# Norm factors in PSUM, priority for bank additions, and a queue order for the next group's operands in a Hymba-style decoder step

## The chip, the cores and the metric

The kernel runs on one core of one Trainium2 chip. A core has five engines that run their own instruction queues and meet through semaphores: TensorE (PE in the profile; PEld is its weight load), VectorE (DVE), ScalarE (ACT), GpSimd (POOL) and SyncE (SP), which here only issues DMAs. [...] The metric is the device time of one execution in microseconds. Lower is better.

## The reference

One decoder layer for 2048 prompt tokens and 8 x 4 sample tokens that share the weights, 2080 token columns in all, with D = 1024 and an FFN width of 2688:

```python
h = rmsnorm(x)
proj = h @ w_in                                  # q, k, v, u
attn = sliding_window_attention(q, k, v)         # window 128, sinks, ALiBi
ssm  = gelu(s5(u));  ssm = ssm * sigmoid(ssm @ w_glu + b_glu)
merged = concat(rmsnorm(attn) * g_attn, rmsnorm(ssm) * g_ssm)
x = x + merged @ w_out
up = rmsnorm(x) @ w_up                           # 2 x 2688 columns
c = conv_b + sum(conv_w[i] * buf[:, i : i + L] for i in range(3))   # causal, buf = state and up
a, g = split(c)
x = x + (silu(g) * a) @ w_down
y = rmsnorm(x) * norm_final
```

Everything is float32. The outputs are y and the new states of attention, S5 and convolution.

## The kernel before

Activations are kept transposed: 128 partitions of one feature block, and token columns along the free dimension. Each float32 matrix product is made of three products of reduced-precision parts: an operand is split into a high part (a cast on one engine, line 84 on ACT) and a low part (source less high part, line 87), and `mm3` (lines 92 to 94) adds high x high, high x low and low x high in one PSUM bank. So every operand that a matmul reads costs a cast and a subtraction on other engines.

The stages follow one another: the projections, attention and S5, GLU, then the output projection, and then the FFN in two groups of four token tiles each, each group with an up-projection of 21 units and a down-projection of 21 blocks for each of its token stretches.

A scheduler orders the instructions of each engine. It takes the program order of the Python text as the priority and issues whatever is ready first; `tc.high_priority(offset=n)` moves instructions n places ahead in that order, and `tc.issue_after(ins)` puts what is traced in its block behind `ins` in the queue of ins's engine, without a wait for its end. Every engine then executes its queue in order, and so does SP with its DMAs.

**Output projection** (lines 1148 to 1175). A loop over eight tiles of 260 columns and, in each, eight output blocks m. A block is 24 matmuls into one of four banks of the pool `ps`. Line 1156 fetches the residual `xm` for the block (12 buffers for 8 blocks a tile), line 1160 adds the bank to it and so frees the bank, and line 1161 stores the sum. Between the blocks three pieces of other work are traced:

- `merged_norm` (line 967) makes the operands of the next tile. For each half of the features `rstd` (line 97) sums the squares over the partitions with a matmul by ones (line 101), takes Ln and Exp on ACT and makes one Newton step on DVE (lines 107, 108, 110); four multiplications (line 975) and four splits follow, whose intermediate `mf` has two buffers.
- `ffn_norm` (line 1123) normalises the finished tile: the same `rstd`, then eight multiplications in place in `xm` (line 1128), each with a store to h2scr (line 1129). Only that store frees the buffer of `xm`.
- `merged_sums` (line 958) loads the inputs of the tile after the next (`mt`, two buffers) and adds their squares on POOL.

The matmul by ones writes to one of two banks of the pool `pst`; the factor itself is in SBUF. Two more banks, the pool `psj`, served earlier stages and lie idle here. In tiles 5 and 6 `early_sums` (line 1101) makes sums and differences of normalised tiles for the first FFN group.

**Up-projection.** `unit` (line 1316) computes one column block of both halves for four tiles. It uses seven products of sums of operands in place of eight: the chain of banks `ux` takes A11, S2, S3 and S1 one after another, the banks `u2`, `u3`, `u4` take A12, S4 and A22. The operands are x0, t2, q1 and q0, each with a high and a low part. `conv` (line 1285) applies the convolution and the gate, and stores the activation to actscr. In the first unit of the first group `finish_front` (line 1187) normalises the last tile; it then closes `pst`, opens the two banks `psv` that u3 uses, and loads q0. In the first unit of the second group `last_norm` does the final norm of the tokens that the first down-projection ended with; its sums use a u3 bank (line 1395).

**Down-projection.** `down` (line 1431) takes the 21 blocks of the FFN width one after another: `load_a` fetches the activation's two parts, `load_wd` (line 1411) a weight, which it splits on ACT and POOL, and 24 matmuls follow. Beside the first group's down-projection the generator `prepare(1)` (line 1485) makes the operands of the second group, one step for each block (line 1474): it loads tiles of h2scr, forms sums on DVE (line 1206 is one of them) and splits them. The cc, ca and cb tiles of the units and the loaded activations share ten buffers of the tag c2.

Of the kernel before, what the change touches and what calls it, by code (L numbers as in the profile page):

```python
# [18 lines left out]
P = 128  # L19
# [61 lines left out]
def split(nc, hi, lo, src, hi_eng, lo_eng):  # L81

    if hi_eng is nc.scalar:
        nc.scalar.copy(hi, src)  # L84
    else:
        hi_eng.tensor_copy(hi, src)
    lo_eng.tensor_tensor(lo, src, hi.bitcast(F32), ALU.subtract)  # L87
# [9 lines left out]
def rstd(c, pool, ps_pool, pstag, ss, n, ones, nm):  # L97
# [13 lines left out]
    return r  # L111

# [515 lines left out]
def body(tc, a):  # L628
# [16 lines left out]
    with ExitStack() as top:  # L645
# [321 lines left out]
        def merged_norm(it, mt, ss, ps_pool, tag):  # L967
# [3 lines left out]
            for half in range(2):  # L971
                r = rstd(c, p3, ps_pool, tag, ss[half], n, ones[512], f"m{half}_{it}")
# [128 lines left out]
        def early_sums(pool, sub, k):  # L1101
# [4 lines left out]
            g, v = nc.gpsimd, nc.vector  # L1106
            g.tensor_tensor(b0[:, 0], b1[:, 0], b0[:, 0], ALU.subtract)
            g.tensor_tensor(t2, b1[:, 1], b0[:, 0], ALU.subtract)
            v.tensor_tensor(b1[:, 0], b1[:, 1], b1[:, 0], ALU.subtract)
            v.tensor_tensor(b0[:, 1], b0[:, 1], t2, ALU.subtract)  # L1110
# [4 lines left out]
        with after_preload():  # L1115
# [7 lines left out]
            def ffn_norm(it, xs, ss):  # L1123
                t0, n = TILES3[it]
                r = rstd(c, p3b, pst, "st", ss, n, ones[1024], f"f_{it}")
# [22 lines left out]
            for it, (t0, n) in enumerate(TILES3):  # L1148
# [5 lines left out]
                for m in range(KD):  # L1154
# [5 lines left out]
                    nc.vector.tensor_tensor(xm, xm, pt[:, :n], ALU.add)  # L1160
                    nc.sync.dma_start(x2scr[:, m, t0 : t0 + n], xm)
                    xs.append(xm)
                    if m == 0 and it == 0:
                        sums = merged_sums(1, p3m)
                    if m == (1 if it else 3) and it + 1 < len(TILES3):
                        nxt = merged_norm(it + 1, *sums, pst, "st")
                    if m == 5 and it + 2 < len(TILES3):
                        sums = merged_sums(it + 2, p3m)
                    if m == 2 and old is not None:
                        ffn_norm(*old)  # L1170
# [91 lines left out]
        def load_q(i):  # L1262
            for sub in range(2):
                q = (ffn.q0, ffn.q1)[i][sub] = hi_lo((hb, hd)[i], [2, 4, W], f"q{i}{sub}", 0)
                for k in range(4):
                    s = c2.tile([P, 2, W], F32, tag="c2", name=f"q{i}r_{sub}_{k}")
                    nc.sync.dma_start(s, qscr[:, sub, i, k])
                    split(nc, *[t[:, :, k] for t in q], s, nc.scalar, nc.vector if i else (nc.gpsimd, nc.vector)[k % 2])
# [16 lines left out]
        def conv(ti, j, half, pt, cc):  # L1285
# [22 lines left out]
            if half:  # L1308
# [4 lines left out]
                nc.vector.tensor_tensor(ca.bitcast(F32R), g, cg, ALU.subtract)  # L1313
                nc.sync.dma_start(actscr[:, j, :, t0 : t0 + n], cc[:, :, :n])

        def unit(gi, j, ws, mid):
# [30 lines left out]
            for s in subs:  # L1347
                v.tensor_tensor(c11[s], c11[s], ca[s][:, 0], ALU.add)
                conv(4 * gi + s, j, 0, c11[s], cc0[s])
            products(chain, s2, [ffn.t2[s] for s in subs], False)  # L1350
            for s in subs:
                nc.scalar.copy(ca[s][:, 1], x[s])
            if mid:
                mid()
            p3 = banks(psv, "u3", "u3")
            products(p3, s4, [half(ffn.q1[s], 1) for s in subs])
# [54 lines left out]
        def load_wd(gi, j, t0):  # L1411
# [16 lines left out]
            split(nc, *w, r, nc.scalar, nc.gpsimd)  # L1428
            return w

        def down(gi, beside):

            old = None
            for ti, (t0, n) in enumerate(TILESD[gi]):
# [5 lines left out]
                def load_a(j):  # L1440
                    hl = [dt([P, n], F32R, f"a{i}_{t0}_{j}") for i in "hl"]
                    for i, t in enumerate(hl):
                        nc.sync.dma_start(t.bitcast(F32), actscr[:, j, 1 - i, t0 : t0 + n])
# [186 lines left out]
```

## Time and profile before

| | us |
|---|---|
| median of 3 runs | 2246.32 (2243.3 to 2248.94) |
| the profiled execution, its own time | 2243.47 |
| its span in the trace | 2241.7 |
| PE busy in the span | 2059.5 (92%) |
| DVE, ACT, POOL busy | 1352.0, 1055.4, 1195.8 |

The stages lie in the span like this: the output projection from 547 to 786 us, the first group's up-projection to 1241, its down-projection to 1505, the second group's up-projection to 1952, and its down-projection to the end. In a timeline a row is start, length, engine, line, operation, output <- inputs, shapes and count; brackets hold the idle time of that engine ahead of the row and what ended it. Times are microseconds, means of groups nanoseconds. A matmul's row is longer than the distance to the next, since matmuls overlap; the distance from start to start is what one costs. The granted clock is the share of full speed that TensorE was given.

### The profile page before, as it was taken

To read this page: it belongs to the slowest core of one execution; us is meant where nothing else is said; L and a number is where in the kernel's file an instruction comes from. 1 tells how busy PE (TensorE), PEld (TensorE's weight loads), DVE (VectorE), ACT (ScalarE), POOL (GpSimd) and SP (SyncE) were. 2 spreads that over 40 slices of the span, in tenths; PEclk is the share of its full clock that TensorE was granted. 3 is DMA by queue.
4 is the path that set the end of the run, shared out by engine and by line. 5 is a ranking of instruction groups with operands and counts; after the bars stand their busy time and mean duration, and the time that the engine had idled before them with its cause. 6 is when DMAs were issued, how large, how long until landed. Compare 5 with 4: busy or idle time off the path is not lost.

```text
span 2241.7 us, 41507 instructions
## 1 busy us (share of the span) xinstructions
PE 2059.5 (92%) x14685; PEld 1931.3 (86%) x14685; DVE 1352.0 (60%) x3326; ACT 1055.4 (47%) x2459; POOL 1195.8 (53%) x1168
## 2 busy tenths in 40 slices
PE   8969999978988879999999799998999999889997
PEld 8967878867888879999999687788999999779897
DVE  8859898357678676667667533318666666600231
ACT  6525555674443256666666332225556655611111
POOL 4847775343445456666666443455666666722211
PEclk9989999989999989999999899999999999989998
DMA  7865434785466663333333784744333333573643
GB/s 234 247 160 148 137 104 121 145 237 177 132 207 215 218 214 95 109 106 112 93 116 112 232 283 137 278 149 152 95 110 105 106 98 103 162 204 108 215 129 98
DMA packets 294352, 347.59 MB, mean 155 GB/s; under 512 B 42344, under 2 KB 250864, under 8 KB 294128
## 3 DMA queue, kind: packets, MB, share of 16 engines
q1 hardware_dynamic: 294144, 344.94, 50.7%
q8 instruction: 116, 1.90, 0.4%
q14 instruction: 92, 0.75, 0.1%
HBM read 232.70 MB, written 107.80 MB: 152 GB/s over the span
## 4 chain that ended last, share of the span: by engine, by line
PE 70%; DVE 11%; DMA 6%; issue 4%; ACT 3%; POOL 3%; SPq 2%; DVEq 0%; POOLq 0%; ACTq 0%
PE ux L1328 20%; PE u L1328 15%; PE dn L93 7%; PE dn L94 7%; PE dn L92 7%; DVE xm L1128 2%; PE qkv L92 1%; PE qkv L93 1%; PE qkv L94 1%; SPq L776 1%; PE wo L92 1%; PE wo L94 1%; PE wo L93 1%; PE o L541 1%; PE tp_b L530 1%
## 5 line engine op out<-in xcount | busy, mean ns | idle before, releaser
L87 POOL TENSOR_TENSOR wdl<-wdr,wdh 128x1024 fp32r<-128x1024 f32 x65 | 158.6, 2444 | 306.0 <-ACT wdh L84 280.9
L92 PE MATMUL dn<-ah,wdh 128*128 128x512 f32 (+3 forms) x552 | 205.1, 372 | 19.7 <-DMA ah<-actscr 16.7
L94 PE MATMUL dn<-ah,wdl 128*128 128x512 f32 (+3 forms) x552 | 205.1, 371 | 2.0 <-POOL wdl L87 1.9
L1480 DVE TENSOR_TENSOR xo<-xo,dn 128x512 f32<-128x512 f32 (+3 forms) x40 | 21.9, 584 | 306.0 <-PE dn L94 305.9
L93 PE MATMUL dn<-al,wdh 128*128 128x512 f32 (+3 forms) x552 | 204.6, 371 | 0.1
L84 ACT CAST wdh<-wdr 128x1024 fp32r<-128x1024 f32 x65 | 68.2, 1050 | 273.7 <-PE dn L93 246.3
L1293 ACT ACTIVATE cc<-u,cw 128x260 f32<-128x260 f32 (+1 forms) x252 | 141.3, 563 | 94.3 <-DVE u L1367 67.2
L92 PE MATMUL wo<-mh,wo 128*128 128x260 f32 x512 | 153.5, 300 | 25.8 <-DVE xm L1160 25.8
L87 POOL TENSOR_TENSOR wls<-s,whs 128x1024 fp32r<-128x1024 f32 x42 | 101.2, 2411 | 130.6 <-ACT whs L84 130.6
L1294 DVE SCALAR_TENSOR_TENSOR cc<-u,cw,cc 128x260 f32<-128x260 f32 (+1 forms) x252 | 120.9, 480 | 66.7 <-ACT cc L1293 65.0
L94 PE MATMUL wo<-mh,wo 128*128 128x260 f32 x512 | 150.5, 294 | 0.0
L93 PE MATMUL wo<-ml,wo 128*128 128x260 f32 x512 | 149.9, 293 | 0.0
L92 PEld LDWEIGHTS dn<-ah,wdh 128*128 128x128 f32 x552 | 104.9, 190 | 37.9 <-DMA ah<-actscr 14.8
L1367 DVE TENSOR_TENSOR u<-u,cb 128x262 f32<-128x262 f32 x84 | 36.5, 435 | 155.5 <-PE u L1328 155.5
L92 PEld LDWEIGHTS wo<-mh,wo 128*128 128x128 f32 x512 | 102.9, 201 | 27.5 <-issue 24.6
L92 PE MATMUL qkv<-hh_p,wqh 128*128 128x256 f32 (+1 forms) x384 | 114.3, 298 | 11.7 <-DVE vs L879 7.0
L87 POOL TENSOR_TENSOR wlt<-s,wht 128x512 fp32r<-128x512 f32 x42 | 54.2, 1290 | 131.0 <-ACT wht L84 69.4
L94 PEld LDWEIGHTS dn<-ah,wdl 128*128 128x128 f32 x552 | 104.7, 190 | 19.6 <-POOL wdl L87 3.1
L93 PEld LDWEIGHTS dn<-al,wdh 128*128 128x128 f32 x552 | 105.0, 190 | 17.6 <-DMA al<-actscr 0.8
L1295 DVE SCALAR_TENSOR_TENSOR cc<-u,cw,cc 128x260 f32<-128x260 f32 (+1 forms) x252 | 119.5, 475 | 0.9
L87 POOL TENSOR_TENSOR wlg<-wur,whg 128x1024 fp32r<-128x1024 f32 x42 | 101.3, 2411 | 27.9 <-ACT whg L84 27.9
L92 PE MATMUL dn<-ah,wd 128*128 128x448 f32 (+2 forms) x288 | 94.7, 329 | 23.2 <-DMA ah<-actscr 19.5
(561 smaller groups left out, 8396.5 us busy)
## 6 DMA issues: line engine op xcount, KB each, us to landing
actscr<-cc SPq DMA_DIRECT2D x168, 260.0 KB, 4.9
wur<-in_w_up SPq DMA_DIRECT2D x84, 512.0 KB, 4.2
wdr<-in_w_down SPq DMA_DIRECT2D x77, 512.0 KB, 3.4
x<-in_xT SPq DMA_DIRECT2D x56, 256.0 KB, 3.9
hs<-h2scr SPq DMA_DIRECT2D x44, 262.0 KB, 4.7
ah<-actscr SPq DMA_DIRECT2D x42, 256.0 KB, 4.1
al<-actscr SPq DMA_DIRECT2D x42, 256.0 KB, 3.8
mt<-mscr SPq DMA_DIRECT2D x16, 520.0 KB, 5.1
```

The source lines that it names most:

```text
L84: nc.scalar.copy(hi, src)
L87: lo_eng.tensor_tensor(lo, src, hi.bitcast(F32), ALU.subtract)
L92: nc.tensor.matmul(ps, w[0], x[0], start=first, stop=False)
L93: nc.tensor.matmul(ps, w[0], x[1], start=False, stop=False)
L94: nc.tensor.matmul(ps, w[1], x[0], start=False, stop=last)
L530: nc.tensor.transpose(tp[:, P * j : P * j + P], ss[kv][:, j, P * ch : P * ch + P], c.ident)
L1128: nc.vector.scalar_tensor_tensor(h, xs[k], g_ffn[:, k : k + 1], r, ALU.mult, ALU.mult)
L1293: nc.scalar.activation(cp, pp[:, 2:], AF.Identity, bias=w[3], scale=w[2])
L1294: nc.vector.scalar_tensor_tensor(cp, pp[:, 1 : npr + 1], w[1], cp, ALU.mult, ALU.add)
L1295: nc.vector.scalar_tensor_tensor(cp, pp[:, 0:npr], w[0], cp, ALU.mult, ALU.add)
L1328: nc.tensor.matmul(pt[:, :W], x[p][:, k], y[q][:, k], start=start and k + i == 0, stop=k == 3 and i == 2, skip_group_check=True)
L1367: v.tensor_tensor(c21[s], c21[s], cb[s][:, 0], ALU.add)
```

## The change

1. `merged_norm` in the output projection (from the second tile on) and `ffn_norm` use the new `rstd_psum`: Ln and Exp share one SBUF tile, the Newton step is done in place in the PSUM bank of the sums, and the multiplications read the factor from that bank. The merged factors use the idle pool `psj`.
2. The bank additions of the output projection get priority. `ffn_norm` is traced behind block 1 instead of block 2, `merged_norm` (from the second tile on) behind block 2 instead of block 1.
3. `early_sums` does all four of its operations on POOL.
4. The splits of `load_q` get priority. `finish_front` is called ahead of the S2 products instead of behind them; `last_norm` is called between the two u3 products instead of ahead of both, and each u3 bank is taken just ahead of its product.
5. In `down`, activations are loaded up to three blocks ahead instead of four. A step of the second group's operands is queued behind the last unit's last DVE instruction, and behind the cast, the subtraction and the last activation load that stand ahead of it in the block.

```diff
+def rstd_psum(c, pool, ps, ss, n, ones, nm):
+    nc = c.nc
+    ps = ps[:, :n]
+    nc.tensor.matmul(ps, ones, ss, start=True, stop=True)
+    r0 = pool.tile([P, n], F32, tag="r0", name=f"r0_{nm}")
+    nc.scalar.activation(r0, ps, AF.Ln, bias=c.eps)
+    nc.scalar.activation(r0, r0, AF.Exp, scale=-0.5)
+    nc.vector.scalar_tensor_tensor(ps, ps, EPS, r0, ALU.add, ALU.mult)
+    nc.vector.scalar_tensor_tensor(ps, ps, -0.5, r0, ALU.mult, ALU.mult)
+    nc.vector.scalar_tensor_tensor(ps, ps, 1.5, r0, ALU.add, ALU.mult)
+    return ps
...
-                r = rstd(c, p3, ps_pool, tag, ss[half], n, ones[512], f"m{half}_{it}")
+                if keep:
+                    pt = ps_pool.tile([P, 512], F32, tag=tag, name=f"st_m{half}_{it}")
+                    r = rstd_psum(c, p3, pt, ss[half], n, ones[512], f"m{half}_{it}")
+                else:
+                    r = rstd(c, p3, ps_pool, tag, ss[half], n, ones[512], f"m{half}_{it}")
...
-            v.tensor_tensor(b1[:, 0], b1[:, 1], b1[:, 0], ALU.subtract)
-            v.tensor_tensor(b0[:, 1], b0[:, 1], t2, ALU.subtract)
+            g.tensor_tensor(b1[:, 0], b1[:, 1], b1[:, 0], ALU.subtract)
+            g.tensor_tensor(b0[:, 1], b0[:, 1], t2, ALU.subtract)
...
-                r = rstd(c, p3b, pst, "st", ss, n, ones[1024], f"f_{it}")
+                r = rstd_psum(c, p3b, pst.tile([P, 512], F32, tag="st", name=f"st_f_{it}"), ss, n, ones[1024], f"f_{it}")
...
-                    nc.vector.tensor_tensor(xm, xm, pt[:, :n], ALU.add)
+                    with tc.high_priority(offset=HPD):
+                        nc.vector.tensor_tensor(xm, xm, pt[:, :n], ALU.add)
...
+                    if m == 1 and old is not None:
+                        ffn_norm(*old)
...
-                    if m == (1 if it else 3) and it + 1 < len(TILES3):
-                        nxt = merged_norm(it + 1, *sums, pst, "st")
+                    if m == (2 if it else 3) and it + 1 < len(TILES3):
+                        nxt = merged_norm(it + 1, *sums, psj, "pj", True)
...
-                    if m == 2 and old is not None:
-                        ffn_norm(*old)
...
-                    split(nc, *[t[:, :, k] for t in q], s, nc.scalar, nc.vector if i else (nc.gpsimd, nc.vector)[k % 2])
+                    with tc.high_priority(offset=HPD):
+                        split(nc, *[t[:, :, k] for t in q], s, nc.scalar, nc.vector if i else (nc.gpsimd, nc.vector)[k % 2])
...
-                nc.vector.tensor_tensor(ca.bitcast(F32R), g, cg, ALU.subtract)
+                ffn.last_dve = nc.vector.tensor_tensor(ca.bitcast(F32R), g, cg, ALU.subtract).ins
...
+            if begin:
+                begin()
             products(chain, s2, [ffn.t2[s] for s in subs], False)
             for s in subs:
                 nc.scalar.copy(ca[s][:, 1], x[s])
-            if mid:
-                mid()
-            p3 = banks(psv, "u3", "u3")
-            products(p3, s4, [half(ffn.q1[s], 1) for s in subs])
+            p3 = []
+            for s in subs:
+                if mid and s:
+                    mid()
+                p3 += [psv[s].tile([P, 512], F32, tag="u3", name=f"u3_{gi}_{j}_{s}")]
+                products(p3[s:], s4, [half(ffn.q1[s], 1)])
...
-            split(nc, *w, r, nc.scalar, nc.gpsimd)
+            ffn.last_act, ffn.last_pool = split(nc, *w, r, nc.scalar, nc.gpsimd)
...
-                        nc.sync.dma_start(t.bitcast(F32), actscr[:, j, 1 - i, t0 : t0 + n])
+                        ffn.last_sp = nc.sync.dma_start(t.bitcast(F32), actscr[:, j, 1 - i, t0 : t0 + n]).ins
...
-                    for ahead in range(i, min(i + 4, NF)):
+                    for ahead in range(i, min(i + 3, NF)):
...
-                        next(beside, None)
+                        with tc.issue_after(ffn.last_dve), tc.issue_after(ffn.last_act), tc.issue_after(ffn.last_pool), tc.issue_after(ffn.last_sp):
+                            next(beside, None)
...
-                unit(gi, j, ws, None if j else last_norm if gi else finish_front)
+                unit(gi, j, ws, None if j or gi else finish_front, last_norm if gi and j == 0 else None)
```

`HPD` is 90. `split` now returns its two instructions.

More of the change, by code (lines that the diff above doesn't have):

```diff
@@ L81, in split @@
 def split(nc, hi, lo, src, hi_eng, lo_eng):
[L83 to L87, printed above, removed]
+    i = nc.scalar.copy(hi, src) if hi_eng is nc.scalar else hi_eng.tensor_copy(hi, src)
+    return i.ins, lo_eng.tensor_tensor(lo, src, hi.bitcast(F32), ALU.subtract).ins
 def mm3(nc, ps, w, x, first, last):
@@ L965, in merged_sums, with merged_norm @@
             return mt, [sumsq(c, p3, mt[4 * h : 4 * h + 4], n, f"m{h}_{it}", nc.gpsimd) for h in range(2)]
-        def merged_norm(it, mt, ss, ps_pool, tag):
+        def merged_norm(it, mt, ss, ps_pool, tag, keep=False):
             n = TILES3[it][1]
@@ L1105, in early_sums @@
             t2 = pool.tile([P, W], F32, tag="t2", name=f"est_{sub}_{k}")
-            g, v = nc.gpsimd, nc.vector
+            g = nc.gpsimd
             g.tensor_tensor(b0[:, 0], b1[:, 0], b0[:, 0], ALU.subtract)
             g.tensor_tensor(t2, b1[:, 1], b0[:, 0], ALU.subtract)
-            v.tensor_tensor(b1[:, 0], b1[:, 1], b1[:, 0], ALU.subtract)
-            v.tensor_tensor(b0[:, 1], b0[:, 1], t2, ALU.subtract)
+            g.tensor_tensor(b1[:, 0], b1[:, 1], b1[:, 0], ALU.subtract)
+            g.tensor_tensor(b0[:, 1], b0[:, 1], t2, ALU.subtract)
             nc.sync.dma_start(t2scr[:, sub, k], t2)
@@ L1312, in conv, with unit @@
                 nc.scalar.copy(cg.bitcast(F32R), g)
-                nc.vector.tensor_tensor(ca.bitcast(F32R), g, cg, ALU.subtract)
+                ffn.last_dve = nc.vector.tensor_tensor(ca.bitcast(F32R), g, cg, ALU.subtract).ins
                 nc.sync.dma_start(actscr[:, j, :, t0 : t0 + n], cc[:, :, :n])
-        def unit(gi, j, ws, mid):
+        def unit(gi, j, ws, begin, mid):
             a11, a12, s2, s4, s3, a22, s1 = ws
```

## The prediction

> **What bounds the kernel now.** I read the busy time by stage, then the waits of TensorE (PE) in the slow stage, then that stage's timeline engine by engine. The first row is the output projection, from its first to its last matmul; columns are stretch, length, busy time of PE, PEld (weight load), DVE (VectorE), ACT (ScalarE) and POOL (GpSimd), granted clock, DMA share and GB/s. The second row is a wait: total, times, longest.
>
> ```profile
> 547.00:786.00 239.00, 208.35 (x1582) 204.87 (x1580) 171.89 (x330) 93.51 (x234) 111.31 (x125) 0.93 0.63 194
> PE wo L92 <- DVE xm L1160: 25.8, 7, 4.8
> ```
>
> PE should be full here and is not: seven times it waits for line 1160, the addition that empties a bank, and the granted clock is 0.93. One such stall, in order of time (start, length, engine, line):
>
> ```profile
> 604.95 0.42 PE L92 MATMUL wo<-mh,wo 128*128 128x260 f32 x1
> 607.77 0.42 PE L93 MATMUL wo<-ml,wo 128*128 128x260 f32 x1
> 608.35 0.28 PE L93 MATMUL wo<-ml,wo 128*128 128x260 f32 x1
> 608.47 0.28 PE L94 MATMUL wo<-mh,wo 128*128 128x260 f32 x1
> 615.22 0.60 PE L101 MATMUL st_f<-ss_f,ones 128*128 128x260 f32 x2
> 614.55 0.43 DVE L107 SCALAR_TENSOR_TENSOR t_m<-st_m,r_m 128x260 f32<-128x260 f32 x1
> 624.05 1.36 DVE L975 SCALAR_TENSOR_TENSOR mf<-mt,vec,rs_m 128x260 f32<-128x260 f32 x2 [0.31 <-POOL ml L87]
> 625.33 6.22 DVE L1128 SCALAR_TENSOR_TENSOR xm<-xm,vec,rs_f 128x260 f32<-128x260 f32 x8
> 625.90 6.00 SPq L1129 DMA_DIRECT2D h2scr<-xm  x8
> 631.95 1.87 SPq L1156 DMA_DIRECT2D xm<-in_xT  x4
> 634.40 0.78 DVE L1160 TENSOR_TENSOR xm<-xm,wo 128x260 f32<-128x260 f32 x2 [1.09 <-DMA xm<-in_xT]
> 634.97 0.56 PE L92 MATMUL wo<-mh,wo 128*128 128x260 f32 x1 [4.79 <-DVE xm L1160]
> ```
>
> This tile starts on PE at about 604.1. The merged norm of the next tile (st_m to mf) comes first, the FFN norm of the old tile (st_f, eight multiplications at 625.33) last. Its stores leave by 631.9, and only behind them does SP fetch four xm tiles, whose buffers those stores free (12 buffers, 8 a tile). The addition at 634.40 waits for that fetch, and PE has waited since 630.18 (634.97 less 4.79). So the chain is old norm, store, refill, addition, bank. After the restart the clock is low: from 604.95 to 607.77 are 13 steps of 0.217 us, against 0.12 from 608.35 to 608.47. Some 15 slow steps cost 15 x 0.097 = 1.5 us. A stall thus costs itself and 1.5 us: 25.8 + 7 x 1.5 = **36.3 us** in the stage.
>
> **Part 1: factors in PSUM.** Means in this stage, by form (busy, mean ns | idle before), and one group of eight from the last tile, where POOL idled from 772.5 to 795:
>
> ```profile
> L1128 DVE SCALAR_TENSOR_TENSOR xm<-xm,vec,rs_f 128x260 f32<-128x260 f32 x56 | 38.8, 761 | 0.0
> L975 DVE SCALAR_TENSOR_TENSOR mf<-mt,vec,rs_m 128x260 f32<-128x260 f32 x56 | 34.4, 651 | 4.8 <-POOL ml L87 4.6
> L1160 DVE TENSOR_TENSOR xm<-xm,wo 128x260 f32<-128x260 f32 x64 | 26.1, 420 | 35.6 <-PE wo L94 18.4 <-DMA xm<-in_xT 17.0
> L108 DVE SCALAR_TENSOR_TENSOR t_f<-t_f,r_f 128x260 f32<-128x260 f32 x7 | 6.2, 881 | 0.0
> L107 DVE SCALAR_TENSOR_TENSOR t_f<-st_f,r_f 128x260 f32<-128x260 f32 x7 | 2.9, 416 | 0.0
> 778.03 3.29 DVE L1128 SCALAR_TENSOR_TENSOR xm<-xm,vec,rs_f 128x260 f32<-128x260 f32 x8
> 795.02 1.10 POOL L1278 TENSOR_TENSOR prevt<-prev,cw 128x336 f32<-128x336 f32 x1 [22.51 <-DVE q11l L87]
> ```
>
> Eight multiplications take 3.29 us with POOL idle and 6.22 beside it. L1160 and L107, which read one operand from PSUM, keep 420 and 416 ns; L108, the same arithmetic with all operands in SBUF, takes 881. So an operation with both tensors in SBUF is held by POOL, and one with a PSUM operand is not. The diff moves r into PSUM, which takes every L1128 and L975 and two of the three factor steps out of this: about 2.9 us per group of eight, and 0.9 per FFN factor chain (0.88 + 0.42 to two of 0.42). The instructions keep their number but one: Ln and Exp now share r0, so the second half's Ln waits for the first half's factor; that lies under four mf. The rows don't show a write of r to PSUM; I take 0.42 us, as L107, with 0.88 as the other end.
>
> [...]
>
> **Part 2: order in the tile.** st_f moves from behind block 2 to behind block 1, the merged norm one block back. Blocks take 24 x 0.12 = 2.9 us, so a warm tile is 8 x 2.9 + 0.6 for the sums' matmuls (st_f's row, 0.60; they overlap their neighbours) = 23.8. From tile start: st_f at 5.8; Ln and Exp by 7.5 (two ACT passes of about 0.4, as L1310's 0.39 below, and the hand-overs); factors by 8.8; eight multiplications by 12.5 with an addition between; last store issued by 13, its refill landed near 15.5. Block 4 ends at 15.5, and PE needs its bank at 23.8. The additions' priority removes the queue ahead of them too. Eight microseconds of room: the bank stall goes.
>
> Next in line is the merged norm: st_m, today ahead of st_f, at 9.0. From t_m at 614.55 to the last mf at 625.41 took 10.9 us beside POOL, nearer 8 without the holding; behind the FFN norm it runs 12.5 to 21, the last ml at 22 against 23.8. Its SBUF tiles mt (two buffers) then refill:
>
> ```profile
> mt<-mscr SPq DMA_DIRECT2D x16, 520.0 KB, 5.1
> ah<-actscr SPq DMA_DIRECT2D x42, 256.0 KB, 4.1
> L1107 POOL TENSOR_TENSOR es<-es,es 128x262 f32<-128x262 f32 x8 | 6.8, 856 | 20.6 <-DMA es<-h2scr 19.1 <-DMA h2scr<-xm 1.5
> ```
>
> Refill 5.1 plus squares and sums of about 4 puts the next tile's second sum at 21 + 9 = 30, 6.2 into a tile that asks for it at 9.0. Under 3 us of room. In tiles 5 and 6 POOL also takes 16 subtractions from DVE, 16 x 0.856 = 13.7 us; there I leave half the stall, and two more us elsewhere: 36.3 - 8 = **28 us** gained in the stage.
>
> **Part 3: the last FFN norm.** It runs in the first up-projection unit:
>
> ```profile
> 799.55 0.60 PE L101 MATMUL st_f<-ss_f,ones 128*128 128x260 f32 x2
> 802.88 0.59 PE L1328 MATMUL u<-q10h,whs 128*128 128x262 f32 x1 [2.73 <-DVE t_f L107]
> 805.69 6.31 DVE L1128 SCALAR_TENSOR_TENSOR xm<-xm,vec,rs_f 128x260 f32<-128x260 f32 x8
> 811.56 0.39 PE L1328 MATMUL u<-q00h,whg 128*128 128x262 f32 x1 [1.07 <-ACT q00h L84]
> 816.11 0.59 PE L1328 MATMUL u<-q00l,whg 128*128 128x262 f32 x1 [4.16 <-POOL q00l L87]
> 787.19 0.36 PE L1328 MATMUL ux<-x00h,whv 128*128 128x262 f32 x1 [1.72 <-DVE xm L1160]
> ```
>
> The statistics move ahead of the S2 products (about 5 us), and the multiplications shorten by 3: q0 can be there 8 us sooner, and 1.07 + 4.16 + 1.5 for the clock go. The price: the u3 bank, freed today by L107, stays with r until the last multiplication. If that lands on the first u3 bank, the 2.73 stays. With a little kept back, **6 us**. The first unit's own wait for the last tile's bank, the chain above once more, also goes: **2 us**.
>
> **Part 4: operands of the second group.**
>
> ```profile
> 1241.67 2.54 DVE L1206 TENSOR_TENSOR hs<-hs,hs 128x262 f32<-128x262 f32 x1
> 1243.94 5.43 SPq L1416 DMA_DIRECT2D wdr<-in_w_down  x2
> 1245.24 0.39 ACT L1310 ACTIVATE u<-cc 128x260 f32<-128x260 f32 x1 [2.89 <-DVE cc L1295]
> 1250.42 0.54 SPq L1443 DMA_DIRECT2D ah<-actscr  x1
> 1255.62 0.80 PE L92 MATMUL dn<-ah,wdh 128*128 128x512 f32 x1 [14.58 <-DMA ah<-actscr]
> 1968.91 0.74 PE L92 MATMUL dn<-ah,wd 128*128 128x448 f32 x1 [16.97 <-DMA ah<-actscr]
> 1426.07 0.50 PE L94 MATMUL dn<-ah,wdl 128*128 128x512 f32 x1 [1.91 <-POOL wdl L87]
> 1440.36 0.63 ACT L84 CAST q01h<-hs 128x524 fp32r<-128x524 f32 x1 [4.23 <-DVE hs L1225]
> ```
>
> In the last unit DVE does L1206 for the next group while its own convolutions wait; ACT's L1310 waits 2.89 for them, a down weight's cast queues behind it, and SP's in-order queue behind that weight's buffer, until ah leaves at 1250.42. Queued behind the unit, L1206 frees 2.5 us and earlier ones some more: **4 us**, bounded by 0 and 7. It can't be the whole 14.58: the second group has nothing beside it and waits 16.97. Behind each down weight, the operand's casts no longer delay the weight's at 1426: 1.91, I take **2**. DVE, ACT, POOL and SP each get the queueing: behind them stand only the next group's loads and splits, wanted by the next units, whose first is at 1516.94 below; their last cast is at 1440.36, long before. Loading three blocks ahead instead of four adds no instruction; blocks take 2.9 us at 256 columns and a load 4.1 (its issue row stands in part 2), so two blocks cover it; nothing, between -3 and +8.
>
> **Part 5: the second group's start.**
>
> ```profile
> 1516.94 1.13 PE L1396 MATMUL st_fo<-ss_fo,ones 128*128 128x512 f32 x2 [2.11 <-DVE ss_fo L122]
> 1520.94 0.39 PE L1328 MATMUL u<-q11h,whs 128*128 128x262 f32 x1 [1.42 <-DVE rs_fo L1401]
> ```
>
> The first u3 product (1.5 us) now covers the first wait, but it used to cover the second: the sums and L1401 end where they did. Nothing, within 1.
>
> **Sum.** 28 + 6 + 2 + 4 + 2 = 42 us. The profiled execution took 2243.47 (span 2241.7), the median is 2246.32; 2246.3 - 42 = **2204**.
>
> **Rivals.** *Half of it*: the merged norm or the SP queue ends last in most tiles and keeps half the stalls, and parts 3 and 4 give 5: 2246 - 18 - 5 = 2223. For it: under 3 us of room. Against: DVE is 172 of 239 us busy and loses some 5 us a tile.
> *Nothing*: the holding stays with r in PSUM. Then the multiplications ahead cost the merged norm 6.2, it ends 6 us late, and PE waits for ml or st_m where it waited for xm: about 2244. Against: 416 beside 881 ns.
> *Slower*: as before, and in tiles 5 and 6 the sums queue behind POOL's 13.7 us of subtractions, so that in-order PE stands at st_m. It decides once st_m is later than the 3.7 us (25.8 / 7) a tile that now is lost; 13.7 over what is there gives 2257.
> *More*: both stages lose every stall, part 4 gives 7: 36 + 10 + 2 + 7 + 4 = 59: 2187.
>
> **Chances.** Forecast 0.58, half 0.22, more 0.10, nothing 0.06, slower 0.04. A measurement tells 0.3% (6.7 us) from no change. Faster 0.90, same 0.06, slower 0.04. The range goes from the far case to a little past half: 2184 to 2230.
>
> **What would show it.** L1128 and L975 near 420 to 490 ns beside POOL; no wait of wo for L1160 above 1 us; the stage near 211 us; q0 waits gone at the first unit; the first down wait near 10 us. Wrong if L1128 stays above 700, if wo waits for ml or st_m, or if ah waits grow in the down blocks.

## The result and the profile after

| | before | after |
|---|---|---|
| median, all runs of both kernels | 2247.63 us (2243.3 to 2255.62, 4 runs) | 2222.76 us (2218.95 to 2224.6, 4 runs) |
| ratio | | 0.9883, 95% interval 0.9852 to 0.9914 |
| profiled execution, span | 2243.47, 2241.7 | 2218.95, 2217.2 |

The change takes 24.9 us off; 2204 was predicted, 42 us less, in a range of 2184 to 2230. Read off the timeline of TensorE (PE) by its own stages, the two profiled executions stand so (us). A group's first unit is counted here up to the second product of the next unit (the one into `u2`), because PE waits there for a bank that the first unit frees:

| stage | before | after | difference |
|---|---|---|---|
| output projection, first to last matmul | 238.2 | 216.4 | -21.8 |
| wait ahead of the first unit | 1.7 | 5.5 | +3.8 |
| first unit | 42.6 | 37.5 | -5.0 |
| rest of the up-projection | 411.3 | 408.5 | -2.8 |
| wait ahead of the first down block | 14.6 | 10.1 | -4.5 |
| first group's down-projection | 249.9 | 256.6 | +6.7 |
| second group's first unit | 34.6 | 32.8 | -1.8 |
| the rest of the span | 701.5 | 700.4 | -1.1 |

The output projection starts 2.0 us later in the second, behind code that the change leaves alone; with this the rows add up to the 24.5 us between the spans.

The line numbers have moved: the bank addition is now L1176 (it was L1160), the FFN multiplications L1143 (L1128) with their stores L1144, the merged multiplications L990 (L975), the fetch of xm L1171, the factor steps L119 to L121, `mm3` L89 to L91. First the stage's row (length, PE, PEld, DVE, ACT, POOL busy, granted clock, DMA share, GB/s):

```profile
549.00:766.00 217.00, 203.50 (x1582) 198.49 (x1581) 137.25 (x311) 90.61 (x232) 115.96 (x141) 0.97 0.70 215
```

DVE is busy for 137 us where it was for 172; some 11 of these 35 us were the 16 subtractions of the early sums (L1109 and L1110, 4.1 and 7.1 us), which POOL does now. The granted clock rose from 0.93 to 0.97. PE's waits from here into the first unit:

```profile
PE ux L1345 <- DVE xm L1176: 5.5, 1, 5.5
PE wo L90 <- POOL ml L84: 3.6, 6, 1.5
PE st_f L115 <- DVE ss_f L133: 3.3, 2, 2.7
PE st_m L115 <- POOL ss_m L133: 3.2, 2, 1.6
PE wo L89 <- ACT mh L83: 2.0, 2, 1.4
PE wo L89 <- DVE xm L1176: 0.9, 1, 0.9
```

The 25.8 us of waits for the addition are 0.9. But waits for ml, mh and st_f have come, 8.9 us together, where one of 0.7 was; st_m waited before too (3.7). In this stage PE now waits for operands and sums, and hardly for banks. DVE's groups in the stage, by form:

```profile
L1176 DVE TENSOR_TENSOR xm<-xm,wo 128x260 f32<-128x260 f32 x64 | 26.6, 418 | 24.3 <-DMA xm<-in_xT 12.3 <-PE wo L91 11.5
L990 DVE SCALAR_TENSOR_TENSOR mf<-mt,vec,st_m 128x260 f32<-128x260 f32 x56 | 25.8, 480 | 13.9 <-POOL ml L84 13.7
L1143 DVE SCALAR_TENSOR_TENSOR xm<-xm,vec,st_f 128x260 f32<-128x260 f32 x56 | 23.4, 480 | 0.2
L119 DVE SCALAR_TENSOR_TENSOR st_f<-st_f,r_f 128x260 f32<-128x260 f32 x7 | 3.0, 427 | 0.0
```

761 and 651 ns have become 480, beside a POOL that is busy for 116 us of the stage where it was for 111; the addition, which read a bank before too, takes 418 for 420, and the second FFN factor step, now in the bank (L120), 436 where with all operands in SBUF it took 881. So in these rows POOL holds the operations with both tensors in SBUF, and hardly those with an operand in PSUM. One tile, which begins on PE at 601.4, in the rows of DVE and of SP's DMAs:

```profile
613.37 0.43 DVE L119 SCALAR_TENSOR_TENSOR st_f<-st_f,r_f 128x260 f32<-128x260 f32 x1
614.77 0.48 DVE L1143 SCALAR_TENSOR_TENSOR xm<-xm,vec,st_f 128x260 f32<-128x260 f32 x1
615.51 2.85 DVE L1143 SCALAR_TENSOR_TENSOR xm<-xm,vec,st_f 128x260 f32<-128x260 f32 x7
616.18 3.38 SPq L1144 DMA_DIRECT2D h2scr<-xm  x7
620.11 1.88 SPq L1171 DMA_DIRECT2D xm<-in_xT  x4
```

The FFN norm now comes first: its last store has left by 619.6, and the refill is on its way at 620.1, where it was at 632 for a tile that began at about the same time. Seven multiplications take 2.85 us, and the eight in the first unit below 3.26, against 3.29 for the eight that POOL left alone before: the PSUM source shows no price here. (The 480 ns are the length of one; neighbours overlap.)

Two waits around the first unit were expected to go or to stay small. First, the unit starts late:

```profile
752.89 2.57 DVE L84 TENSOR_TENSOR t21l<-t2r,t21h 128x524 fp32r<-128x524 f32 x1
755.38 2.62 DVE L133 TENSOR_TENSOR ss_f<-ss_f,sq_f 128x260 f32<-128x260 f32 x1
757.92 0.43 DVE L119 SCALAR_TENSOR_TENSOR st_f<-st_f,r_f 128x260 f32<-128x260 f32 x1
765.04 1.89 SPq L1171 DMA_DIRECT2D xm<-in_xT  x4
767.45 0.77 DVE L1176 TENSOR_TENSOR xm<-xm,wo 128x260 f32<-128x260 f32 x2 [3.46 <-DMA xm<-in_xT]
771.17 0.56 PE L1345 MATMUL ux<-x00h,whv 128*128 128x262 f32 x1 [5.49 <-DVE xm L1176]
```

In the last tile splits of t2 and a sum, each of two SBUF tensors and stretched to 2.6 us (0.63 and 0.43 with POOL idle, at 770.94 and 770.26), stand ahead of the FFN norm; factor, stores, refill and addition follow late, the old chain once more. The second wait is inside the unit:

```profile
780.25 0.38 ACT L1359 COPY ca<-ux 128x262 f32<-128x262 f32 x1 [5.22 <-POOL prev L1298]
783.71 0.48 ACT L117 ACTIVATE r_f<-st_f,eps 128x260 f32<-128x260 f32 x1
784.80 0.44 DVE L119 SCALAR_TENSOR_TENSOR st_f<-st_f,r_f 128x260 f32<-128x260 f32 x1
786.22 3.26 DVE L1143 SCALAR_TENSOR_TENSOR xm<-xm,vec,st_f 128x260 f32<-128x260 f32 x8
789.62 0.56 PE L1345 MATMUL u<-q10h,whs 128*128 128x262 f32 x1 [7.22 <-DVE xm L1143]
```

PE waits 7.2 us for the u3 bank that holds the factor, where it waited 2.7; the two q0 waits of 1.07 and 4.16 are gone in return. Last, the first group's down-projection; the first row is its first matmul, the second the start of its second token stretch:

```profile
1227.38 0.79 PE L89 MATMUL dn<-ah,wdh 128*128 128x512 f32 x1 [10.13 <-DMA ah<-actscr]
1353.54 0.47 PE L89 MATMUL dn<-ah,wdh 128*128 128x512 f32 x1 [3.93 <-DMA ah<-actscr]
1377.88 0.51 PE L91 MATMUL dn<-ah,wdl 128*128 128x512 f32 x1 [1.63 <-POOL wdl L84]
1403.32 0.80 PE L91 MATMUL dn<-ah,wdl 128*128 128x512 f32 x1 [1.70 <-POOL wdl L84]
```

### The profile page after: what moved, and what is told of

The parts are those of the page before. It is cut to its first block, busy times and chain, and to the rows that moved or that the text cites. A ratio compares the mean times of both kernels' runs of the same rounds, so it can differ in the third digit from the quotient of the medians.

```text
span 2217.2 us, 41459 instructions
## 1 busy us (share of the span) xinstructions
PE 2055.2 (93%) x14685; PEld 1926.3 (87%) x14685; DVE 1323.1 (60%) x3310; ACT 1054.1 (48%) x2459; POOL 1200.4 (54%) x1184
## 4 chain that ended last, share of the span: by engine, by line
PE 70%; DVE 10%; DMA 7%; POOL 4%; issue 4%; ACT 3%; SPq 2%; DVEq 0%; POOLq 0%; ACTq 0%
PE ux L1345 20%; PE u L1345 16%; PE dn L90 7%; PE dn L91 7%; PE dn L89 6%; DVE xo L1427 1%; PE wo L90 1%; PE wo L91 1%; PE wo L89 1%; PE qkv L89 1%; DMA y<-yscr 1%; PE qkv L91 1%; PE qkv L90 1%; DMA al<-actscr 1%; SPq L787 1%
## 5 line engine op out<-in xcount | busy, mean ns | idle before, releaser
L89 PE MATMUL dn<-ah,wdh 128*128 128x512 f32 (+3 forms) x552 | 205.7, 373 | 17.1 <-DMA ah<-actscr 14.1
L91 PE MATMUL dn<-ah,wdl 128*128 128x512 f32 (+3 forms) x552 | 205.8, 373 | 3.3 <-POOL wdl L84 3.3
L89 PE MATMUL wo<-mh,wo 128*128 128x260 f32 x512 | 149.8, 293 | 2.9 <-ACT mh L83 2.0
L91 PE MATMUL wo<-mh,wo 128*128 128x260 f32 x512 | 147.1, 287 | 0.0
L89 PEld LDWEIGHTS dn<-ah,wdh 128*128 128x128 f32 x552 | 105.6, 191 | 35.4 <-DMA ah<-actscr 10.3
L89 PE MATMUL qkv<-hh_p,wqh 128*128 128x256 f32 (+1 forms) x384 | 114.7, 299 | 13.6 <-DVE vs L890 8.5
L91 PEld LDWEIGHTS dn<-ah,wdl 128*128 128x128 f32 x552 | 105.5, 191 | 20.9 <-POOL wdl L84 4.2
L84 POOL TENSOR_TENSOR wlg<-wur,whg 128x1024 fp32r<-128x1024 f32 x42 | 101.6, 2419 | 28.1 <-ACT whg L83 28.1
L89 PE MATMUL dn<-ah,wd 128*128 128x448 f32 (+2 forms) x288 | 95.0, 330 | 23.0 <-DMA ah<-actscr 19.3
L90 PE MATMUL qkv<-hl_p,wqh 128*128 128x256 f32 (+1 forms) x384 | 111.1, 289 | 0.0
```

Of the source, the lines that this page charges most:

```text
L84: return i.ins, lo_eng.tensor_tensor(lo, src, hi.bitcast(F32), ALU.subtract).ins
L89: nc.tensor.matmul(ps, w[0], x[0], start=first, stop=False)
L90: nc.tensor.matmul(ps, w[0], x[1], start=False, stop=False)
L91: nc.tensor.matmul(ps, w[1], x[0], start=False, stop=last)
```

## The experiments

All start from the changed kernel. The table gives the output projection, the wait ahead of the first unit together with that unit, and the whole run less that of the kernel before in the same set of runs. Of the experiments all but norm_early ran once, with one run of the kernel before beside each set. Eleven runs of the kernel before on one chip lie between 2243.4 and 2253.7 us, so the difference of two single runs is sure to some 10 us only, and stages carry the argument. The output projection is the same code in six of the profiles (after, last_sbuf, begin_early, prev_first, ahead4, no_queue): 216.4 to 222.4, mean 220.0. So a stage is sure to some 3 us, and the 21.8 of the first table are nearer 18, taken from the only profile of the kernel before.

| kernel | output projection | wait + first unit | whole less before |
|---|---|---|---|
| before | 238.2 | 44.3 | 0 |
| after | 216.4 | 43.0 | -24.9 |
| factors_sbuf | 224.4 | 44.2 | -25.8 |
| old_order | 225.1 | 38.4 | -29.6 |
| priority_alone | 244.5 | 43.9 | -3.8 |
| no_priority | 218.9 | 42.3 | -26.0 |
| early_dve | 222.6 | 41.8 | -28.2 |
| memset_pool | 219.7 | 44.2 | -29.0 |
| last_sbuf | 221.4 | 45.4 | -26.7 |
| begin_early | 219.3 | 50.2 | -28.1 |
| prev_first | 221.8 | 40.6 | -30.4 |
| norm_early | 219.9 | 39.7 | -30.5 |
| ahead4 | 218.5 | 43.1 | -25.0 |
| no_queue | 222.4 | 43.0 | -19.7 |

**Which part frees the bank?** The factors back in SBUF, in the new order:

```diff
-                r = rstd_psum(c, p3b, pst.tile([P, 512], F32, tag="st", name=f"st_f_{it}"), ss, n, ones[1024], f"f_{it}")
+                r = rstd(c, p3b, pst, "st", ss, n, ones[1024], f"f_{it}")
...
-                        nxt = merged_norm(it + 1, *sums, psj, "pj", True)
+                        nxt = merged_norm(it + 1, *sums, psj, "pj")
```

> The changed kernel with all norm factors back in SBUF (same order, priorities, pools, queueing). Theory (holding): the multiplications of both norms go from 480 ns back to 650 to 760, the factor steps from 430 to 530 to 880, DVE has some 20 us more in the output projection, and the merged norm becomes late: the stage (216 us from first to last matmul) grows by 10 to 25 us, with waits for ml or st_m. The first unit's u3 wait falls from 7.2 to about 3. Rival (order alone): the order of the two norms made the gain; the stage stays within 4 us of 216 although the multiplications are slow.

The stage takes 224.4, 8 us above the changed kernel's profile and 4 above the mean, so between theory and rival. There is no wait for the addition at all; the waits for ml grew. Its waits and its multiplications:

```profile
PE wo L90 <- POOL ml L84: 8.0, 9, 2.2
PE st_f L98 <- DVE ss_f L133: 4.6, 4, 1.5
```

```profile
L990 DVE SCALAR_TENSOR_TENSOR mf<-mt,vec,rs_m 128x260 f32<-128x260 f32 x56 | 33.2, 620 | 9.5 <-POOL ml L84 8.9
L1143 DVE SCALAR_TENSOR_TENSOR xm<-xm,vec,rs_f 128x260 f32<-128x260 f32 x56 | 28.5, 570 | 0.2
```

So the new order frees the bank also with multiplications that POOL holds, though these are not as slow as before (570 ns for 761). (In the first unit the u3 wait falls to 1.1 us, and q0 is late by 3.6 and 2.5.) Then the old order with the factors in PSUM:

```diff
-                    if m == 1 and old is not None:
-                        ffn_norm(*old)
...
-                    if m == (2 if it else 3) and it + 1 < len(TILES3):
+                    if m == (1 if it else 3) and it + 1 < len(TILES3):
...
+                    if m == 2 and old is not None:
+                        ffn_norm(*old)
```

> The FFN norm of the old tile goes back behind the third block and the next tile's merged norm back behind the second; the PSUM factors, the priority of the additions and everything else stay. Theory (the order made most of the gain; with the factors in SBUF the stage took 224.4 us and no bank wait came back): the chain of stores, refill and addition is late again, the waits of wo for the addition come back with at least 10 of the 25.8 us, and the stage takes 228 to 236 us; whole run 2234 to 2243. Rival (priority and the faster arithmetic are enough in either order): bank waits under 5 us, the stage 216 to 223, and the run within 5 us of the changed kernel.

225.1: the bank waits did come back, 18.0 us of them, and yet the stage is only 5 us longer than the mean, since nothing else waits but st_m (3.5); and the first unit with the wait ahead of it comes out 4.6 us better. Theory and rival each missed half. Over both stretches the old order takes 263.5 us, and the kernels with the new order and the same first unit (after, ahead4, no_queue) 259.4 to 265.4: with the factors in PSUM the new order shows no gain of its own. To see whether the priority, which the last two kernels share, made the gain, both parts were undone together, the two edits above in one; of it here the merged norm:

```diff
                     with tc.high_priority(offset=HPD):
                         nc.vector.tensor_tensor(xm, xm, pt[:, :n], ALU.add)
...
-                    if m == (2 if it else 3) and it + 1 < len(TILES3):
-                        nxt = merged_norm(it + 1, *sums, psj, "pj", True)
+                    if m == (1 if it else 3) and it + 1 < len(TILES3):
+                        nxt = merged_norm(it + 1, *sums, psj, "pj")
```

> Of the change in the output projection only the priority of the additions is left (with the two subtractions on POOL): factors in SBUF, the merged norm first and the FFN norm behind the third block, as before. Before, the stage took 238.2 us; PSUM factors and priority in the old order took 225.1, new order and priority with SBUF factors 224.4, all three 216 to 222. Theory (order and PSUM factors are two ways to the same end, each worth some 13 us without the other, and the priority little): the stage takes 233 to 239 us with 20 us or more of bank waits, the run 2240 to 2255. Rival (the priority is what the two kernels have in common and made the 13 us): the stage takes 222 to 228, the bank waits stay near the 18 us of the old order, and the run ends within 6 us of 2226.

The stage is at 244.5, above the 238.2 of before. Its waits of wo, and its multiplications; then the waits of old_order:

```profile
PE wo L89 <- DVE xm L1176: 33.3, 6, 9.0
```

```profile
L1143 DVE SCALAR_TENSOR_TENSOR xm<-xm,vec,rs_f 128x260 f32<-128x260 f32 x56 | 40.0, 780 | 0.0
```

```profile
PE wo L89 <- DVE xm L1176: 18.0, 6, 4.1
```

From 244.5 the PSUM factors alone take 19.4 us, the order alone 20.1, both 24.5 (to the mean of 220.0): two ways to the same end. What made the stage 6 us longer than before (the priority, or POOL's two more subtractions in the tiles that run up to the wait of 9.0) was not told apart; the subtractions are not all of it, for the waits at 637 and 668 were longer already (5.6 and 5.0 us, before 4.8 and 3.5), and the first early sum is at 675.7. From the changed kernel the priority alone was then taken out:

```diff
-                    with tc.high_priority(offset=HPD):
-                        nc.vector.tensor_tensor(xm, xm, pt[:, :n], ALU.add)
+                    nc.vector.tensor_tensor(xm, xm, pt[:, :n], ALU.add)
```

> The additions of the output projection lose their priority; order, PSUM factors and all else stay. Theory (with the FFN norm first the additions have time enough): the stage stays at 216 to 223 us, with under 5 us of waits for the addition. Rival (without it the additions queue on DVE behind eight multiplications and the statistics, and free their banks late): 5 to 15 us of bank waits, the stage 226 to 235 us.

218.9 and no wait for the addition: in the new order the priority shows no effect.

**What are the new waits?** POOL's two more subtractions go back to DVE:

```diff
-            g.tensor_tensor(b1[:, 0], b1[:, 1], b1[:, 0], ALU.subtract)
-            g.tensor_tensor(b0[:, 1], b0[:, 1], t2, ALU.subtract)
+            v.tensor_tensor(b1[:, 0], b1[:, 1], b1[:, 0], ALU.subtract)
+            v.tensor_tensor(b0[:, 1], b0[:, 1], t2, ALU.subtract)
```

> Of the four subtractions of each early sum, the two that the change gave to POOL go back to DVE; all else stays. Theory (POOL is not late in the two tiles with early sums, DVE loses 16 operations): DVE is held up more, some 16 x 0.5 to 0.8 us = 8 to 13 us more busy in these two tiles, but it waits there for the buffer anyway, so the stage stays within 3 us of 216 to 222. Rival (POOL's 13.7 us of subtractions are what makes the sums and ml late from 628 to 687): the waits of wo for ml in that stretch, 7 us in all, go away, and the stage is 4 to 7 us shorter, 210 to 214.

```profile
PE wo L90 <- POOL ml L84: 6.0, 9, 1.7
```

The stage takes 222.6 and the waits for ml stay, so it is not these two subtractions alone. Next, a wait that stands in DVE's queue in the changed kernel, 4.87 and 2.92 us ahead of the memset of L1102:

```diff
-                nc.vector.memset(s[:, :, NSMP : NSMP + 2], 0.0)
+                (eng or nc.vector).memset(s[:, :, NSMP : NSMP + 2], 0.0)
...
-            b0 = stage(pool, "b0", sub, k, 4, "es0")
+            b0 = stage(pool, "b0", sub, k, 4, "es0", nc.gpsimd)
```

> The small memset of the early sums' first buffer goes from DVE to POOL; all else stays. Theory (DVE stands in order at this memset until a buffer's store has left, 4.87 us at 664 and 2.92 at 669, and so the FFN norm and the merged norm behind it are late): the two DVE waits go, the waits of wo for mh and ml from 681 to 687 (3.7 us and the slow clock behind them) go or fall under 1 us, the stage takes 4 us less than without it. Rival (POOL is late there anyway): the same waits stay, now behind POOL, and the stage is unchanged within 2 us.

The rival held: the stage takes 219.7, as the mean. DVE's two waits went, and its FFN norm ended by 668.4; but the wait moved with the memset:

```profile
670.00 0.10 POOL L1102 MEMSET es<- 128x4 f32 x1 [2.67 <-DMA qscr<-es]
674.01 0.76 POOL L1122 TENSOR_TENSOR es<-es,es 128x262 f32<-128x262 f32 x1 [3.91 <-DMA es<-h2scr]
...
680.23 0.48 DVE L990 SCALAR_TENSOR_TENSOR mf<-mt,vec,st_m 128x260 f32<-128x260 f32 x1 [8.14 <-POOL ml L84]
```

POOL stands in its queue for a buffer and then for a load of the early sums; behind the load come 5.5 us of its own sums and subtractions (674.0 to 679.5) and only then ml, and with two buffers of mf DVE waits 8.1 us for ml. PE's waits for mh and ml from 682 to 690 are no shorter than in the changed kernel. In the tile at 714 the sums of squares are late in the same way, in the changed kernel:

```profile
714.52 0.42 ACT L129 ACTIVATE ss_m<-mt 128x260 f32<-128x260 f32 x1 [1.90 <-DMA mt<-mscr]
714.85 1.02 ACT L132 ACTIVATE sq_m<-mt 128x260 f32<-128x260 f32 x3
716.22 0.98 DVE L133 TENSOR_TENSOR ss_f<-ss_f,sq_f 128x260 f32<-128x260 f32 x1 [2.86 <-ACT sq_f L132]
```

ACT waits 1.9 us for the load of mt, and the FFN's square sq_f stands behind it; st_f then waits 2.66 at 720.16. That was read, not tried.

**The bank in the first unit.** The last norm's factor alone back in SBUF:

```diff
+                if it == len(TILES3) - 1:
+                    r = rstd(c, p3b, pst, "st", ss, n, ones[1024], nm)
+                else:
+                    r = rstd_psum(c, p3b, pst.tile([P, 512], F32, tag="st", name=f"st_{nm}"), ss, n, ones[1024], nm)
```

> The changed kernel with the last tile's FFN factor (the one made in the first up-projection unit) back in SBUF; all else as changed. Theory (bank): the 7.2 us wait of the first u3 product is the PSUM bank that the factor now holds until the last of the eight multiplications; with the factor in SBUF the first factor step frees it and the wait falls to about 3 us (784.80 + 0.44 against 782.40), while the eight multiplications go from 3.3 to 4 to 6 us and q0 comes up to 3 us later, which the s4 and s3 products (6 us) cover. First unit some 3 to 4 us shorter. Rival (late statistics): the wait is set by the late Ln and Exp and stays near 7; the unit is not shorter.

```profile
789.83 0.58 PE L1349 MATMUL u<-q10h,whs 128*128 128x262 f32 x1 [2.88 <-DVE t_f L104]
797.77 0.39 PE L1349 MATMUL u<-q00h,whg 128*128 128x262 f32 x1 [0.42 <-ACT q00h L83]
802.06 0.58 PE L1349 MATMUL u<-q00l,whg 128*128 128x262 f32 x1 [3.90 <-POOL q00l L84]
```

The bank is free at the first factor step and the wait is 2.9; but q0 now is late by 0.4 and 3.9, and the unit takes 40.0 where the changed kernel takes 37.5. In factors_sbuf and priority_alone, where this factor is in SBUF too, it takes 39.6 and 40.4; in the six other experiments whose unit is the changed kernel's, 35.5 to 38.7. So holding the bank is the cheaper side, by 2 to 3 us. Then the norm was begun earlier:

```diff
+            if begin:
+                begin()
             c11 = [t[:, :W] for t in p2]
...
-            if begin:
-                begin()
             products(chain, s2, [ffn.t2[s] for s in subs], False)
```

> The last FFN norm is begun in the first up-projection unit ahead of the additions and convolutions of its first quarter instead of behind them; same instructions. Theory (its factor steps stand on DVE from 777.4 to 784.8 behind the convolutions, and the bank that r holds is free only behind the last multiplication at 789.5): the statistics are on PE already, so the eight multiplications end some 4 to 5 us sooner, the wait of the third quarter's products falls from 7.2 to 2 to 4 us, and the unit's 37.5 us to 32 to 34. Rival (the additions and convolutions put behind the norm are needed as soon): PE waits as long for them, in u2's bank or later, and the unit stays at 36 to 39 us.

```profile
784.92 0.44 DVE L119 SCALAR_TENSOR_TENSOR st_f<-st_f,r_f 128x260 f32<-128x260 f32 x1 [2.32 <-ACT r_f L118]
789.74 0.56 PE L1345 MATMUL u<-q10h,whs 128*128 128x262 f32 x1 [5.15 <-DVE xm L1143]
805.31 0.56 PE L1345 MATMUL u<-q00h,whg 128*128 128x262 f32 x1 [7.00 <-DVE cc L1323]
```

The wait fell to 5.2, and the rival was right with more than it asked: the unit takes 44.8. DVE is free and waits for Ln and Exp, for ACT stands at the copy into ca (5.2 us for POOL, as at 780.25 in the changed kernel). And the convolutions, now behind the norm and q0's splits, keep their bank 7 us too long. So POOL's block was moved ahead of the loads of q1:

```diff
-        load_q(1)
         tailp = up.tile([P, 2 * NF, 2], F32, tag="tailp", name="tailp", bufs=1)
...
         gq.tensor_tensor(prev[:, :, :, 1], prev[:, :, :, 1], wide(3), ALU.add)
+        load_q(1)
```

> The block that loads the earlier steps' convolution inputs and computes with them on POOL is written ahead of the loads of q1 instead of behind them; same instructions. Theory (the last norm is late at the first unit because ACT stands 5.2 us, from 775.0 to 780.2, at the copy into ca, whose buffer that block on POOL holds; Ln and Exp queue behind it, so that the factor is ready only at 785.3 though the sum of squares is there at 776.3): the 5.2 us at the copy go, the factor steps start 2.5 to 4 us sooner, the wait of the third quarter's products falls from 7.2 to 3 to 5 us, and the unit from 37.5 to 34 or 35 us. Rival (the factor steps wait for DVE's convolutions ahead of them in any case): the wait stays at 6.5 to 7.5 us.

```profile
778.18 0.64 ACT L1359 COPY ca<-ux 128x262 f32<-128x262 f32 x2
784.35 0.48 ACT L117 ACTIVATE r_f<-st_f,eps 128x260 f32<-128x260 f32 x1
785.45 0.44 DVE L119 SCALAR_TENSOR_TENSOR st_f<-st_f,r_f 128x260 f32<-128x260 f32 x1
790.27 0.56 PE L1345 MATMUL u<-q10h,whs 128*128 128x262 f32 x1 [5.64 <-DVE xm L1143]
```

The 5.2 us at the copy are gone and the unit takes 35.6, but Ln still stands on ACT behind the convolutions and, at 782.72, a table load of 1.28 us (ACT_TABLE_LOAD): half of the theory, half of the rival. Both moves (of the norm without the loads of q0), with the splits of t2 traced later:

```diff
+                    if it == len(TILES3) - 1 and m == 3:
+                        load_t2()
...
-            with after_preload():
-                ffn_norm(*old)
             pst_close()
...
+            if begin:
+                with after_preload():
+                    ffn_norm(*old)
             c11 = [t[:, :W] for t in p2]
```

> Three moves in one, read stage by stage. (1) The split of t2 goes from the end of the seventh tile to behind the fourth block of the last one; theory: on DVE the splits t21l (2.44 and 2.57 us) and the sum behind them (2.62) stand ahead of the last tile's FFN norm, so its refill lands at 767.4 and the first unit waits 5.5 us; without them that wait falls to 0 to 2.5 us; rival (the refill is late on SP's queue anyway): it stays over 4. (2) The block of earlier convolution inputs ahead of the loads of q1, as in the run of that move alone, where the 5.2 us at the copy into ca went but the factor steps then stood behind DVE's convolutions, and (3) the last norm alone, without the loads of q0, ahead of these convolutions; theory: only both together start the factor early: the wait of the third quarter falls from 7.2 to 1 to 3.5 us and the unit from 37.5 to 32 to 34; rival (the convolutions are needed as soon): a wait for a bank or for cc takes its place, 36 or more. Whole run by the theory 8 to 10 us under the changed kernel, a ratio to before of 0.983 to 0.985; by the rivals 0.988 to 0.990.

Median 2219.9 (6 runs), before 2250.36 (11 runs), ratio 0.9872, interval 0.9849 to 0.9895: no different from the changed kernel's 0.9883. The unit takes 34.4 and its bank wait 3.7, a little outside the theory's figures. The wait ahead of it stayed:

```profile
758.77 1.01 DVE L84 TENSOR_TENSOR t21l<-t2r,t21h 128x524 fp32r<-128x524 f32 x1
759.71 2.63 DVE L133 TENSOR_TENSOR ss_f<-ss_f,sq_f 128x260 f32<-128x260 f32 x1
762.26 0.42 DVE L119 SCALAR_TENSOR_TENSOR st_f<-st_f,r_f 128x260 f32<-128x260 f32 x1
```

But the scheduler put the splits ahead of the factor as before, so the 5.3 us there say nothing of the theory; it is open.

**The down-projection.** Four blocks ahead again, and then the next group's steps without the queueing:

```diff
-                    for ahead in range(i, min(i + 3, NF)):
+                    for ahead in range(i, min(i + 4, NF)):
```

> The changed kernel with activations loaded up to four blocks ahead in the down-projection again; the queueing of the next group's operands stays. The first group's down blocks (first to last matmul) grew from 249.9 to 256.6 us. Theory P (prefetch): three ahead is what costs it; with four they return to about 250, the wait at the second stretch from 3.9 to about 2.2, and the second group's waits for ah and al (2.8 and 2.3) to 2.5 and 1.8. Theory Q (queueing): they stay near 256. The wait between the last unit and the first block (10.1 + 1.4) stays under 12 by P if queueing made it, and returns toward 14.6 if three ahead made it.

```diff
-                        with tc.issue_after(ffn.last_dve), tc.issue_after(ffn.last_act), tc.issue_after(ffn.last_pool), tc.issue_after(ffn.last_sp):
-                            next(beside, None)
+                        next(beside, None)
```

> The changed kernel without the queueing of the next group's operands; three blocks ahead stays. Theory Q: the down blocks return from 256.6 to about 250 and the wait at the first block goes from 10.1 + 1.4 back to about 14.6. Theory P: blocks stay near 256, and if the shorter wait comes from the prefetch it stays near 11.

| | rest of up | wait | down-projection | sum |
|---|---|---|---|---|
| before | 411.3 | 14.6 | 249.9 | 675.8 |
| after | 408.5 | 10.1 | 256.6 | 675.3 |
| ahead4 | 408.6 | 10.8 | 254.1 | 673.5 |
| no_queue | 409.8 | 15.0 | 251.1 | 675.9 |

Without the queueing the wait is back at 15.0, as theory Q said: the queueing takes 4 to 5 us from it. (The 1.3 of the up-projection are not surely its own; last_sbuf, which has it, takes 410.0.) The blocks give part of it back, and four blocks ahead do not prevent that: over the twelve profiles with the queueing they take 249.2 to 256.6 us, mean 253.4, against 249.9 and 251.1 without it. The sum is 668.2 to 675.3 there, mean 672.5; so the queueing is worth some 3 us, at the edge of what these profiles can tell. In the changed kernel PE waits 11.8 us inside the blocks, before 7.1, and the granted clock there is 0.96 for 0.98. Why the blocks take longer is open: the second stretch's wait for ah was 3.9 in the changed kernel and 5.8 with four ahead, against 2.2 before, but 2.1 in last_sbuf, which has the queueing and three ahead. The waits for wdl near 1377 (1.6) come without the queueing too.

## Why the prediction was right, and where its sizes were off

- **The mechanism held**: the bank wait of the output projection was the largest loss, it went, and the result lies within the range. The size did not: 24.9 us are 0.6 of the 42. They are what the half case gave (2223), whose reasons hold in part: the merged norm does end last, but it kept none of the old stalls and brought new ones, and Parts 3 and 4 gave little together. That its number was met so closely is partly luck.
- **Part 1** was right of the operations (480 and 427 ns beside POOL), and the PSUM source showed no price (eight multiplications in 3.26 us, for 3.29 from SBUF with POOL idle). The write to PSUM costs what L119 shows, 0.43. One sum in it was wrong, and nothing was built on it: 0.88 + 0.42 to two of 0.42 saves 0.46 us a factor chain, not 0.9.
- **Part 2**, the order, was right that the refill would come in time, but not with eight microseconds of room: the forecast had it landed 15.5 us into the tile, and it only starts 15.8 us into the second tile and 18.8 to 24.7 into the later ones, which last 25 to 31. By old_order the new order was also not needed beside the factors in PSUM, which the sum did not see. The term that was mis-sized is the stage's 28 us, with 8 kept back for what is late next: 8.9 us of waits for ml, mh and st_f came, and the gain is 18 to 22. PE's waits in the stage fell from 30.2 to 13.0 us, which leaves at most some 5 of the 21.8 for the clock, where the forecast had 10.5. "Under 3 us of room" for the merged norm was the right place. What is late from 655 to 690 is not only the subtractions given to POOL (forecast as 13.7 us, measured 10.8; moving them back showed no gain) but also in-order waits for loads and buffers, on POOL as the memset's run shows, and on ACT by the rows at 714.
- **Part 3**: "the 2.73 stays" became 7.2: the bank was priced by the multiplications alone, and not by the factor's own lateness, behind ACT's copy and DVE's convolutions. The q0 waits went as said, and the unit gained 5.0 of the 6, but not by that account: what the bank took back, the 1.7 at S2 (for a copy into ca) and 1.1 at the next unit's bank made up in part. "The first unit's own wait" fell to the other side: +3.8 for -2; by the rows the factor of the last tile but one is late on DVE, which the run with the later splits could not test.
- **Part 4**: the wait ahead of the down blocks came out as said (near 10), but the forecast counted it as a gain and in these two profiles the blocks give back more than it (+6.7 for -4.5). The 2 us for the wait at 1426 were wrong: it is still there, 1.70 at 1403.
- **Part 5**: nothing was forecast, and nothing is shown: the 1.8 us of this profile come in six of the thirteen profiles with the change (32.7 to 32.8), and in the other seven the stretch takes 34.5 to 34.6 as before.
- **The rivals' sums**: the slower case's 2257 is 13.7 on the profiled run; on the median, from which the other cases start, it is 2260.

Two of the signs that would show it wrong came up: wo waits for ml, and the wait for ah in a down block grew. They rightly told of a smaller gain, not of a loss.

## What to carry to other kernels

Two cures for one stall do not add up: here, from the kernel with neither, each alone took some 20 of the 24 us, so cost the second against what the first leaves. When a stall goes, the room behind it is the next bound (here 8.9 us of waits came up behind the 25.8); count what stands in order on the engine that makes the next operand, its waits for loads and buffers included, and not only its busy time. A buffer that also carries a result is held from the first producer's lateness to the last reader's end (here PE waited 7.2 us for it, and 2.7 before); price both ends.

## What the runs showed unexpectedly

- How far POOL can stretch a DVE operation on two SBUF tensors: in the changed kernel a 128x524 subtraction took 0.63 us with POOL idle (four in 2.54 at 770.94) and 2.57 beside it, a 128x260 sum 0.43 (at 770.26) and 2.62. The sum began at 755.38 beside one POOL subtraction that ran from 754.85 to 757.71, and ended at 758.00: it seems to have stood until that one ended, where the multiplications of the stage had lost only 0.3 us each on average.
- The same code in the same stage differed by 6 us between profiles (216.4 to 222.4), and the kernel before by 12 us between chips and runs (2243.3 to 2255.6). A single pair of profiles does not size a term of 3 us.
